# Routing lists written group by group, and the first expert's weight splits placed behind the routing

## The chip, the cores and the metric

The kernel runs on one core of one Trainium2 chip. The metric is the device time of one execution in microseconds (us). The engines are named as in the profile: PE multiplies matrices, DVE (vector), ACT (scalar) and POOL work on tiles in SBUF, and SP only issues DMAs. POOL issues the indirect DMAs (gathers and scatters by an index), which the profile lists as its instructions.

## The reference, cut to what matters

One block of a network on 2048 tokens of width 1024, all in float32: two mixers, then a mixture of experts. Only the part from the second norm on matters here.

```python
x = x + gt1 * (mixed @ w_out[l])
h2 = rmsnorm(x, norm2_g[l]) * (1.0 + sc2) + sh2
x = x + gt2 * hier_moe(h2, ...)          # and a last rmsnorm

# hier_moe: 4 groups of 8 experts, two experts for each token
lg = (xf @ wg_r) + bg_r                  # 4 group logits
grp_idx = top_k(lg, 1)
le = ((xf @ we_r) + be_r)                # 32 expert logits
pe = softmax(le of the chosen group)
top_p, top_i = lax.top_k(pe, TOP_K)
wts = p_grp * top_p / sum(top_p)
...
hid = silu(xblk @ w_gate[e]) * (xblk @ w_up[e])
yb = hid @ w_down[e]                     # for each expert and its tokens
out = out.at[buf_tok].add(yb * buf_w)
```

## The kernel before, in words

The program has three parts one after the other: the mixers, a middle part (class `Mid`), and the experts (class `Moe`). The change lies at the border of the last two.

**The middle part** goes over 16 tiles of 128 tokens. `Mid.tile(i)` multiplies a tile with `w_out` on PE (48 products of 128x512, because each float32 operand is split into a high and a low part and three of the four products are kept), scales the result on DVE (line 934, tile `wot`) and adds it to `x` (line 935, on POOL, for the last tile on DVE). `Mid.after(j)` stores `x`, transposes it on PE, copies the transposes on ACT (line 948), takes the sum of squares on ACT (line 951), the reciprocal root on DVE and POOL (`rsqrt_small`, lines 86 and 87, tile `xrs`), forms the 36 logits `lg` (line 956 on PE, line 957 on DVE) and the normed row `h` (lines 958 and 959 on DVE), which is stored to `H2`.

**The routing** (`route`) takes a group of tiles, `GROUPS = [(0, 4), (4, 4), (8, 4), (12, 2), (14, 1), (15, 1)]` as (first tile, count). It is a chain of some fifty short DVE instructions from `lg` to the two one-hot choices `E` and their sum `M` (line 1057), two small products on PE (lines 1062 and 1063) that count how many tokens went to each expert before, and then the destination index `di` (line 1073) for each of the two choices. For each tile of the group and each choice it writes 128 rows of 16 bytes into the DRAM tensor `LIST` with one indirect DMA from POOL (line 1081): 32 such writes in all.

**The weights.** An expert has 12 pieces of 128x1024 float32 (4 of gate, 4 of up, 4 of down), 512 KB each. `Moe.load_next` issues the load of the next piece into a `raw` buffer. `Moe.pump(n)` splits the next n pieces into high and low parts (`halves`, line 1239 on ACT into `whi`, line 1240 on DVE into `wlo`), and each split issues the next load. There are 7 `raw` buffers, 12 pairs of `whi` and `wlo`, and 8 more raw buffers (`raw2`) once the memory of the middle part is free. `Moe.first`, called behind `tile(15)`, issues 7 loads and splits all 12 pieces of expert 0, with 12 more loads.

**The order.** Up to the end of `Mid.run` a planner orders the instructions of each engine, by the place in the program and by its own estimate of times. From `Moe.run` on each engine goes in the order of the program. `Moe.run` reads the lists of experts 0 to 2 on SP (line 1371, which waits for all writes of `LIST`), clears three buffers `gx` (line 1376, which also waits for those writes, since the buffers lie in memory that the routing used), takes the counts, gathers the rows of expert 0, 1 and a second block of expert 0 (line 1244), transposes and splits them (lines 1255, 1260, 1261), issues 8 loads on ACT's DMA queue, and starts the loop over the experts. In expert 0's `block` the first two pieces are used, then the hook `mid` runs an extra block for expert 0's tokens past 128 (tiles `ih`, `il`), which uses all 12 pieces, and then its own block goes on.

Of the kernel before, what the change touches and what calls it, by code (L numbers as in the profile page):

```python
# [864 lines left out]
class Mid:  # L865
# [103 lines left out]
    def run(s, ctx):  # L969
        s.moe.lasting()  # L970
        s.k.md = s.t = ctx.enter_context(s.k.tc.tile_pool(name="md", bufs=1, side="right"))
        s.rows()
        s.consts()
        xs, n, due = s.xs, len(s.xs), []
        for i in range(n, 17):
            if i < 15:
                s.tokens(i + 1)
            if i < 16:
                xs[i] = s.tile(i)
            if i == 15:  # L980
                s.moe.first()
            for j in [j for j in sorted(xs) if j < i]:
                i0, c = [(i0, c) for i0, c in GROUPS if i0 <= j < i0 + c][0]
                if j == i0:
                    lg = s.t.tile([128, 4, 36], FP, name="lg", bufs=4)
                s.after(j, xs.pop(j), lg[:, j - i0])
                if j == i0 + c - 1:
                    due.append((i0, c, lg))
                if due and (j >= sum(due[0][:2]) - 1 + (0 if due[0][0] > 8 else 3)):
                    route(s.k, *due.pop(0), s.moe.ps)  # L990
        for d in due:
            route(s.k, *d, s.moe.ps)


def first_of_max(k, v, mx, n, name):
# [12 lines left out]

def route(k, i0, c, lg, ps):

    nc, md = k.nc, k.md
    T = lambda n, *sh: md.tile([128, 4, *sh], FP, name=n, bufs=4)[:, :c]
    gl, el = lg[:, :c, 0:4], lg[:, :c, 4:36]
    gm = T("gm"); nc.vector.tensor_reduce(gm, gl, AX.X, OP.max)
# [52 lines left out]
    for j, e in enumerate(E):  # L1067
        t = T("pt" + str(j), 32); nc.vector.tensor_tensor(t, pos, e, OP.mult)
        d = T("d" + str(j)); nc.vector.tensor_reduce(d, t, AX.X, OP.add)
        if j == 1:  # L1070
            nc.vector.tensor_tensor(d, d, aside, OP.add)
        di = md.tile([128, 4], I32, name="di" + str(j), bufs=4)[:, :c]
        nc.vector.tensor_copy(di, d)
        row = md.tile([128, 4, 4], FP, name="lrow" + str(j), bufs=4)[:, :c]
        rowi = row.bitcast(I32)
        nc.gpsimd.iota(rowi[:, :, 0], pattern=[[128, c]], base=i0 * 128, channel_multiplier=1)
        nc.gpsimd.iota(rowi[:, :, 1], pattern=[[128, c]], base=i0 * 128, channel_multiplier=1)
        nc.gpsimd.memset(row[:, :, 3], 0.0)
        nc.gpsimd.tensor_scalar(row[:, :, 2], W[j], 1.0, 0.0, op0=OP.mult, op1=OP.add)
        for i in range(c):  # L1080
            one = nc.gpsimd.indirect_dma_start(
                out=k.LIST, out_offset=bass.IndirectOffsetOnAxis(ap=di[:, i:i + 1], axis=0),
                in_=row[:, i], in_offset=None)

            for other in k.scat:
                k.tc.declare_no_dep(one.ins, other.ins, reason="other rows")
            k.scat.append(one)


class Moe:  # L1090
# [31 lines left out]
    def first(s):  # L1122

        for _ in range(min(s.RAW, len(s.todo))):
            s.load_next()
        s.pump(s.RING)

    def load_next(s, queue=None):
        if s.loaded < len(s.todo) and (s.summed or s.loaded < s.k.NE * 12):
# [231 lines left out]
    def run(s, O):  # L1361
        k, nc, tc = s.k, s.nc, s.tc
# [6 lines left out]
        rows = k.LIST[0:65536, :].rearrange("(e a p) c -> p e a c", e=32, p=128)  # L1369
        for e in range(min(NE, 3)):  # L1370
            nc.sync.dma_start(lists[:, e], rows[:, e, 0:4])
        more = {}

        s.gx = [s.t.tile([128, 1024], FP, name=f"gx{j}") for j in range(3)]
# [3 lines left out]
        def second(e):  # L1378

            more[e] = x = s.gx[2]  # L1380
            n = nc.values_load(s.cnt[0:1, e:e + 1], engines=[mybir.EngineType.Pool], min_val=0, max_val=2048)
            with tc.If(n > 128):
                s.gather(lists[:, e, 1], x)

        def first(e):
            x = s.gx[e % 2]
            s.gather(lists[:, e, 0], x)
            return x
        s.counts()
        xs = [first(0)]  # L1390
        if NE > 1:
            xs.append(first(1))
        hl = s.x_tiles()
        for q in range(2):
            s.x_split(s.x_turn(xs[0], q), *hl, q)
        for _ in range(s.LATE):
            s.load_next(nc.scalar)
        second(0)
        for e in range(NE):
            n = nc.values_load(s.cnt[0:1, e:e + 1], min_val=0, max_val=2048)  # L1400
# [49 lines left out]
        with tc.If(most > 128):  # L1450
            for e in (NE - 2, NE - 1):
                n = nc.values_load(s.cnt[0:1, e:e + 1], min_val=0, max_val=2048)
# [118 lines left out]
```

## Time and profile before

| what | us |
|---|---|
| median of 3 runs | 2954.5 |
| lowest and highest of the runs | 2951.3 and 2956.52 |
| the profiled execution | 2948.01 |
| its span from first to last instruction | 2946.2 |

The profiled execution has 1.8 us around its span. Its rows are in a section of their own below; times in them are counted from the start of the span. PE is the busiest engine (2724.7 us, 92% of the span), DVE follows with 2013.0 us (68%), and the DMA engines are busy nearly all of the time while the experts run.

### The profile page before, as it was taken

What the parts mean: (1) busy time and instruction counts of PE and PEld (TensorE: products, weight loads), DVE (VectorE), ACT (ScalarE), POOL (GpSimd) and SP (SyncE); (2) the same over time, 40 slices, a digit from 0 to 9 for tenths busy, and PEclk for the clock granted to TensorE, in tenths of its full rate; (3) what the DMA queues carried; (4) which work ended last, traced back from release to release, by engine and by line L of the source; (5) the groups of instructions that cost most, each with busy time, mean ns of one, the idle gap of its engine ahead of it and who ended that gap; (6) DMA issues with size and microseconds to landing.
All of it is one profiled execution on the core that took longest, in us unless ns stands there. A gap on an engine that the chain in (4) does not pass through costs nothing. (4 is left out here: it accounts for less than half of the span.)

```text
span 2946.2 us, 45527 instructions
## 1 busy us (share of the span) xinstructions
PE 2724.7 (92%) x15434; PEld 2245.7 (76%) x15434; DVE 2013.0 (68%) x4136; ACT 1274.6 (43%) x2183; POOL 798.2 (27%) x983
## 2 busy tenths in 40 slices
PE   6989999999999999999999999899958999999993
PEld 5767787878888888888888878688857777777772
DVE  6374775683676656587647886436565699988984
ACT  4333443342333523333333544322225577767763
POOL 2011322322332312342233343322341112111111
PEclk9989999999999999999999989999979999999996
DMA  8999775577565776566665767976448799999996
GB/s 268 305 335 286 236 236 166 181 240 230 158 209 183 235 240 206 179 219 206 203 198 172 233 207 255 345 271 216 144 151 257 272 364 367 362 331 370 366 320 249
DMA packets 460586, 734.25 MB, mean 249 GB/s; under 512 B 115553, under 2 KB 277345, under 8 KB 460242
## 3 DMA queue, kind: packets, MB, share of 16 engines
q1 hardware_dynamic: 448114, 696.68, 70.7%
q0 software_dynamic: 10976, 29.21, 4.3%
q10 hardware_dynamic: 1152, 4.19, 0.4%
q8 instruction: 164, 2.69, 0.4%
q14 instruction: 180, 1.47, 0.2%
HBM read 561.81 MB, written 175.00 MB: 250 GB/s over the span
## 5 line engine op out<-in xcount | busy, mean ns | idle before, releaser
L778 PE MATMUL mm<-hThi,w 128*128 128x512 f32 x1472 | 592.8, 403 | 16.0 <-ACT hThi L667 10.0
L780 PE MATMUL mm<-hThi,w 128*128 128x512 f32 x1472 | 589.5, 401 | 0.2 <-DVE w L761 0.2
L779 PE MATMUL mm<-hTlo,w 128*128 128x512 f32 x1472 | 588.2, 400 | 0.0
L1240 DVE TENSOR_TENSOR wlo<-raw,whi 128x1024 fp32r<-128x1024 f32 x404 | 483.0, 1252 | 45.3 <-ACT whi L1239 29.2
L1239 ACT CAST whi<-raw 128x1024 fp32r<-128x1024 f32 x408 | 405.6, 1057 | 204.0 <-PE U L931 47.9
L778 PEld LDWEIGHTS mm<-hThi,w 128*128 128x128 f32 x1472 | 280.4, 190 | 85.2 <-ACT hThi L667 10.1
L780 PEld LDWEIGHTS mm<-hThi,w 128*128 128x128 f32 x1472 | 280.4, 191 | 65.2 <-DVE w L761 6.6
L779 PEld LDWEIGHTS mm<-hTlo,w 128*128 128x128 f32 x1472 | 280.2, 190 | 57.4 <-DVE hTlo L668 0.7
L1340 POOL DMA_INDIRECT X<-y,lists x32 | 70.8, 2213 | 484.7 <-DVE y L1332 447.5
L243 DVE TENSOR_TENSOR pr<-Pl,Nl 128x2 f32<-128x2 f32 (+30 forms) x496 | 184.9, 373 | 11.7
L451 POOL TENSOR_TENSOR Xq<-h,kf 128x256 f32<-128x256 f32 x96 | 80.1, 834 | 379.7 <-ACT h L448 128.8
L761 DVE TENSOR_TENSOR w<-wraw,w 128x512 fp32r<-128x512 f32 x108 | 80.5, 746 | 106.6 <-ACT w L760 106.6
L760 ACT CAST w<-wraw 128x512 fp32r<-128x512 f32 x108 | 66.6, 619 | 163.4 <-DMA wraw<-in_w_in_dram 103.7
L244 DVE TENSOR_REDUCE Pl<-pr 128x1 f32<-128x2 f32 (+30 forms) x496 | 124.3, 251 | 12.6
L296 PE MATMUL xy<-UV,Gc 128*64 128x64 f32 (+1 forms) x1536 | 115.3, 225 | 3.0 <-ACT UV L305 3.0
L1270 PE MATMUL G<-whi,xh 128*128 128x512 f32 x256 | 104.1, 407 | 11.3 <-PEq L1413 8.6
L296 PEld LDWEIGHTS xy<-UV,Gc 128*64 128x64 f32 (+1 forms) x1536 | 97.2, 128 | 20.2 <-issue 5.9
L856 PE MATMUL mm<-hThi,w 128*128 128x512 f32 x256 | 104.1, 410 | 7.6 <-DMA w<-Ww_proj_b 2.6
L857 PE MATMUL mm<-hTlo,w 128*128 128x512 f32 x256 | 103.9, 406 | 2.6 <-DVE hTlo L668 2.6
L858 PE MATMUL mm<-hThi,w 128*128 128x512 f32 x256 | 102.3, 400 | 0.0
L1270 PE MATMUL G<-whi,xl 128*128 128x512 f32 x256 | 100.7, 393 | 0.0
L1270 PE MATMUL G<-wlo,xh 128*128 128x512 f32 x256 | 100.6, 393 | 0.0
(495 smaller groups left out, 5798.9 us busy)
## 6 DMA issues: line engine op xcount, KB each, us to landing
raw<-in_exp_w_gate_dram SPq DMA_DIRECT2D x126, 512.0 KB
raw<-in_exp_w_up_dram SPq DMA_DIRECT2D x126, 512.0 KB
raw<-in_exp_w_down_dram SPq DMA_DIRECT2D x124, 512.0 KB
w<-Whg SPq DMA_DIRECT2D x96, 512.0 KB
w<-Wgt SPq DMA_DIRECT2D x96, 512.0 KB
w<-Wrw SPq DMA_DIRECT2D x84, 512.0 KB
wraw<-in_w_in_dram SPq DMA_DIRECT2D x92, 256.0 KB
Whg<-w SPq DMA_DIRECT2D x32, 512.0 KB
```

The lines of the kernel that those rows point to most:

```text
L243: nc.vector.tensor_tensor(pv, Pl[:, :ni, :ns], Nl[:, :ns, t_][:, None, :].to_broadcast([128, ni, ns]), OP.mult)
L244: nc.vector.tensor_reduce(Pl[:, :ni, t_], pv, AX.X, OP.add)
L296: mm = lambda *a_, **kw: nc.tensor.matmul(*a_, skip_group_check=True, **kw)
L778: nc.tensor.matmul(pt, whi, hi[kk // 2][:, kk % 2], start=(kk == 0), stop=False)
L779: nc.tensor.matmul(pt, whi, lo[kk // 2][:, kk % 2], start=False, stop=False)
L780: nc.tensor.matmul(pt, wlo, hi[kk // 2][:, kk % 2], start=False, stop=(kk == 7))
L856: nc.tensor.matmul(pt, w[:, 0, kk], hi[o // 2][:, o % 2], start=(kk == 0), stop=False)
L857: nc.tensor.matmul(pt, w[:, 0, kk], lo[o // 2][:, o % 2], start=False, stop=False)
L858: nc.tensor.matmul(pt, w[:, 1, kk], hi[o // 2][:, o % 2], start=False, stop=(kk == 3))
L1239: s.nc.scalar.copy(hi, raw)
L1240: eng.tensor_tensor(lo, raw, hi.bitcast(FP), OP.subtract)
L1270: mm = lambda *a, **kw: nc.tensor.matmul(*a, skip_group_check=True, **kw)
```

## The change

It does four things. The routing of the groups of four tiles comes one tile behind the group's last tile instead of three, and with `while` instead of `if` several groups can be routed in one step. `route` no longer issues its writes of `LIST` itself but returns them; they are issued right behind the routing, except for tile 14, whose two writes come behind `after(15)`. `Moe.first` only issues its 7 loads; the 12 splits of expert 0 go into `Moe.run`, six ahead of the split of the gathered rows and six behind it. The 8 loads into `raw2` go from ACT's queue, behind the split of the gathered rows, to SP's, right behind the reads of the lists. With this, those 8 loads are pieces 7 to 11 of expert 0 and 0 to 2 of expert 1; before they were pieces 7 to 11 of expert 1 and 0 to 2 of expert 2.

```diff
--- before.py
+++ after.py
@@ -971,7 +971,7 @@
         s.k.md = s.t = ctx.enter_context(s.k.tc.tile_pool(name="md", bufs=1, side="right"))
         s.rows()
         s.consts()
-        xs, n, due = s.xs, len(s.xs), []
+        xs, n, due, rows = s.xs, len(s.xs), [], []
         for i in range(n, 17):
             if i < 15:
                 s.tokens(i + 1)
@@ -986,10 +986,13 @@
                 s.after(j, xs.pop(j), lg[:, j - i0])
                 if j == i0 + c - 1:
                     due.append((i0, c, lg))
-                if due and (j >= sum(due[0][:2]) - 1 + (0 if due[0][0] > 8 else 3)):
-                    route(s.k, *due.pop(0), s.moe.ps)
-        for d in due:
-            route(s.k, *d, s.moe.ps)
+
+                while due and (j >= sum(due[0][:2]) - 1 + (0 if due[0][0] > 8 else 1)):
+                    rows += route(s.k, *due.pop(0), s.moe.ps)
+                if j < 14 or j == 15:
+                    for r in rows:
+                        r()
+                    rows = []
 
 
 def first_of_max(k, v, mx, n, name):
@@ -1008,7 +1011,7 @@
 
 def route(k, i0, c, lg, ps):
 
-    nc, md = k.nc, k.md
+    nc, md, out = k.nc, k.md, []
     T = lambda n, *sh: md.tile([128, 4, *sh], FP, name=n, bufs=4)[:, :c]
     gl, el = lg[:, :c, 0:4], lg[:, :c, 4:36]
     gm = T("gm"); nc.vector.tensor_reduce(gm, gl, AX.X, OP.max)
@@ -1078,13 +1081,15 @@
         nc.gpsimd.memset(row[:, :, 3], 0.0)
         nc.gpsimd.tensor_scalar(row[:, :, 2], W[j], 1.0, 0.0, op0=OP.mult, op1=OP.add)
         for i in range(c):
-            one = nc.gpsimd.indirect_dma_start(
-                out=k.LIST, out_offset=bass.IndirectOffsetOnAxis(ap=di[:, i:i + 1], axis=0),
-                in_=row[:, i], in_offset=None)
-
-            for other in k.scat:
-                k.tc.declare_no_dep(one.ins, other.ins, reason="other rows")
-            k.scat.append(one)
+            def write(di=di[:, i:i + 1], row=row[:, i]):
+                one = nc.gpsimd.indirect_dma_start(
+                    out=k.LIST, out_offset=bass.IndirectOffsetOnAxis(ap=di, axis=0), in_=row, in_offset=None)
+
+                for other in k.scat:
+                    k.tc.declare_no_dep(one.ins, other.ins, reason="other rows")
+                k.scat.append(one)
+            out.append(write)
+    return out
 
 
 class Moe:
@@ -1123,7 +1128,6 @@
 
         for _ in range(min(s.RAW, len(s.todo))):
             s.load_next()
-        s.pump(s.RING)
 
     def load_next(s, queue=None):
         if s.loaded < len(s.todo) and (s.summed or s.loaded < s.k.NE * 12):
@@ -1369,6 +1373,8 @@
         rows = k.LIST[0:65536, :].rearrange("(e a p) c -> p e a c", e=32, p=128)
         for e in range(min(NE, 3)):
             nc.sync.dma_start(lists[:, e], rows[:, e, 0:4])
+        for _ in range(s.LATE):
+            s.load_next()
         more = {}
 
         s.gx = [s.t.tile([128, 1024], FP, name=f"gx{j}") for j in range(3)]
@@ -1391,10 +1397,11 @@
         if NE > 1:
             xs.append(first(1))
         hl = s.x_tiles()
+
+        s.pump(s.RING // 2)
         for q in range(2):
             s.x_split(s.x_turn(xs[0], q), *hl, q)
-        for _ in range(s.LATE):
-            s.load_next(nc.scalar)
+        s.pump(s.RING - s.RING // 2)
         second(0)
         for e in range(NE):
             n = nc.values_load(s.cnt[0:1, e:e + 1], min_val=0, max_val=2048)
```

## Rows read from the trace of the kernel before

**Rows 1.** The page's first line.

```profile
span 2946.2 us, 45527 instructions
```

**Rows 2.** Stages: window, length, busy PE, PEld, DVE, ACT, POOL, then clock, DMA share, GB/s.

```profile
2140.00:2165.20 25.20, 25.20 (x134) 21.45 (x133) 19.82 (x40) 9.64 (x14) 9.89 (x17) 1.00 0.55 182
2165.20:2182.50 17.30, 9.55 (x65) 8.82 (x63) 15.44 (x58) 7.90 (x14) 0.55 (x1) 0.69 0.97 352
2182.50:2205.40 22.90, 4.72 (x18) 4.21 (x18) 10.15 (x100) 0.42 (x2) 16.90 (x25) 0.50 0.06 18
2205.40:2214.50 9.10, 1.90 (x8) 1.58 (x9) 1.94 (x5) 0.58 (x1) 3.98 (x4) 0.50 0.42 103
```

**Rows 3.** Line 1081 on POOL by window: count, ns min/median/max, first and last start.

```profile
L1081 POOL DMA_INDIRECT LIST<-lrow,di x16: 954/958/1072, 2182.5 to 2202.9; - x16
...
L1081 POOL DMA_INDIRECT LIST<-lrow,di x8: 955/964/1070, 2132.3 to 2141.3; - x8
```

**Rows 4.** Timeline of POOL: start, length, engine, line, operation, [idle before, releaser].

```profile
2142.32 1.30 POOL L935 TENSOR_TENSOR raw<-raw,wot 128x512 f32<-128x512 f32 x1
...
2207.92 1.06 POOL L1244 DMA_INDIRECT gx<-H,lists  x1 [1.47 <-DMA lists<-LIST]
```

**Rows 5.** Timeline of SP: the reads of the lists.

```profile
2205.37 1.41 SPq L1371 DMA_DIRECT2D lists<-LIST  x3
```

**Rows 6.** Line 1240 on DVE, 2160 to 2176 us: the splits.

```profile
L1240 DVE TENSOR_TENSOR wlo<-raw,whi x9: 1205/1223/1225, 2161.6 to 2173.4; 128x1024 fp32r<-128x1024 f32 x9
```

**Rows 7.** Timeline of DVE from the last tile's add to its last index.

```profile
2169.56 0.69 DVE L935 TENSOR_TENSOR raw<-raw,wot 128x512 f32<-128x512 f32 x1
...
2176.94 0.25 DVE L957 SCALAR_TENSOR_TENSOR lg<-tr,xrs,rtb 128x36 f32<-128x36 f32 x1 [1.26 <-PE tr L956]
...
2178.68 1.22 DVE L959 TENSOR_TENSOR h<-h,B 128x1024 f32<-128x1024 f32 x1
...
2194.09 0.19 DVE L1057 TENSOR_TENSOR M<-E,E 128x32 f32<-128x32 f32 x1
...
2197.55 0.15 DVE L1073 CAST di<-d 128x1 int32<-128x1 f32 x1 [0.26 <-DVE d L1071]
```

**Rows 8.** Timeline of DVE: eleven routing steps of tiles 8 to 11, first and last.

```profile
2134.55 0.19 DVE L1026 TENSOR_REDUCE m<-le 128x4 f32<-128x32 f32 x1
...
2137.04 0.19 DVE L1034 SCALAR_TENSOR_TENSOR pq<-o1q,pe 128x32 f32<-128x32 f32 x1
```

**Rows 9.** Timeline of PE: the last product of stage one.

```profile
2164.82 0.40 PE L932 MATMUL Y<-whi,wlo 128*128 128x512 f32 x1
```

**Rows 10.** Timeline of PE: the start of the experts.

```profile
2212.61 1.95 PE L1255 MATMUL tr<-ident,gx 128*128 128x128 f32 x8 [16.28 <-DMA gx<-H,lists]
...
2220.55 0.50 PE L1270 MATMUL tr<-whi,il 128*128 128x512 f32 x1
```

**Rows 11.** Timeline of ACT and its DMA queue there.

```profile
2217.97 0.46 ACTq L1167 DMA_DIRECT2D raw<-in_exp_w_gate_dram  x1
2219.18 1.07 ACT L1260 CAST ih<-tr 128x512 fp32r<-128x512 f32 x2 [4.00 <-DMA raw<-in_exp_w_down_dram]
```

**Rows 12.** Timeline of DVE there, and five splits later.

```profile
2205.67 0.91 DVE L1376 MEMSET gx<- 128x1024 f32 x1 [7.97 <-DMA LIST<-lrow,di]
...
2214.48 1.42 DVE L1261 TENSOR_TENSOR xl<-tr,xh 128x512 fp32r<-128x512 f32 x2 [6.73 <-ACT xh L1260]
...
2219.80 1.29 DVE L1261 TENSOR_TENSOR il<-tr,ih 128x512 fp32r<-128x512 f32 x2 [3.90 <-ACT ih L1260]
...
2253.45 5.77 DVE L1240 TENSOR_TENSOR wlo<-raw,whi 128x1024 fp32r<-128x1024 f32 x5
```

**Rows 13.** Line 1244, the gathers of expert rows, over the whole span (columns as rows 3).

```profile
L1244 POOL DMA_INDIRECT gx<-H,lists x36: 985/1410/2057, 2207.9 to 2845.3; - x36
```

**Rows 14.** DMA queues, 2249 to 2250 us: packets, MB, share of 16 engines.

```profile
q0 software_dynamic: 51, 0.21, 53.3%
q1 hardware_dynamic: 47, 0.18, 47.3%
```

## The prediction

> **What bounds the kernel now.** The first view is the table of stages around the border between the middle part and the experts, since the change touches nothing else [rows 2]. To 2165.2 us PE is busy without a gap (25.20 of 25.20 us): it sets the pace, and DVE, POOL or DMA work saved there is worth nothing. Then PE has almost nothing to do for 49 us: 9.55, 4.72 and 1.90 us of work in stretches of 17.3, 22.9 and 9.1 us. So at this border a chain of waits sets the end, and what it gives up comes off the end, as long as the experts start with the same pieces loaded. The second view is the timeline of each engine through that gap, followed back from the first product of the experts:
> - PE waits for the gathered rows until 2212.61 [rows 10], POOL's gather (2207.92) for the lists [rows 4], SP's read of them (2205.37) for all writes of LIST [rows 5].
> - The writes are POOL's. Sixteen of the 32 stand in one train, first start 2182.5, last 2202.9, so 1.36 us apart and the last ending at 2203.9 [rows 3]. POOL is busy 16.90 of 22.9 us there [rows 2].
> - The train is late because tiles 8 to 15 all get their destinations on DVE in this gap, and DVE runs nine splits of 1.22 us in it first (2161.6 to 2173.4) [rows 6]. The last tile's add runs at 2169.56 though its product ended at 2165.22 [rows 9]; its logits come at 2176.94, its M at 2194.09, its last index ends at 2197.70 [rows 7].
>
> **The change part by part.** I follow tile 15 to the end of its writes, then expert 0's start.
>
> *Product to logits.* Without splits on DVE the scaling and the add follow the product at once: two of 0.69 us and a hop of 0.1, so x is whole at 2166.7 instead of 2170.25, 3.5 us sooner. From there to the logits took 6.7 us, with casts of the splits among ACT's work. The bounds of what that loses are 0 and 2.7 us; I take 2, because ACT still has the square and two copies to do. Logits at 2171.4, 5.5 sooner.
>
> *Logits to M.* It took 17.15 us, with the routing of three more groups and the normed row h on DVE in between. Undisturbed, eleven chained steps start within 2.49 us, one round trip to ACT included: 0.25 us each [rows 8]. I count 32 chained steps, 8.0 us, and add h, which the program has ahead of the routing, with two instructions of about 1.25 us [rows 7]: 10.5 us, so 6.6 us less. Bounds: 8.0 (h falls beside) to 15 (tile 14's routing and unexplained pauses of DVE stay).
>
> *M to the last index.* 3.6 us [rows 7], unchanged: two products, five short steps.
>
> *Last index to last write.* It took 6.2 us since five writes still stood in the train. With the twelve writes of tiles 8 to 13 gone earlier and tile 14's two done, tile 15's two remain, 1.27 each, the first from an index that is ready 0.5 us sooner: 1.9 us, so 4.3 less. If tile 14's stand right ahead it is 2.5 more.
>
> Sum so far: 5.5 + 6.6 + 4.3 = 16.4 us; the last write ends at 2187.5. Bounds: 7 (logits held, M at 15 us) and 20.
>
> *The writes that move.* Twelve writes of 1.27 us go into POOL's queue while PE runs tiles 14 and 15, ahead of adds and reciprocal roots there. The trace shows such a burst: eight writes, 2132.3 to 2142.3 [rows 3], held an add to 2142.32 [rows 4], and PE still had no gap [rows 2]. I cost them at nothing; the cover is that PE takes up the transposes only after the next tile's products, and if it were gone the price is up to the 10 us of a burst. The four writes of tiles 12 and 13 (5.1 us) can stand ahead of tile 15's reciprocal root; that is in the bound of 7.
>
> *Expert 0's start*, counted from SP's read of the lists (2205.37 before). Before: DVE's first clear at 0.3, the gather at 2.55, the rows on PE at 7.24, xl from 9.11 to 10.53, il at 14.43, the extra block's third product, which needs il, at 15.18 [rows 4, 5, 10, 12]. The first six splits now stand on DVE behind the clears, because these wait for the writes: two clears of 0.91 end at 2.3, and six splits at 5.77/5 = 1.15 us [rows 12] end at 9.2. ACT's casts run ahead of that. The rows come later by two things. POOL prepares the gather beside splits: gathers take from 0.985 to 2.057 us, median 1.410 [rows 13], and the one here, beside an idle DVE, took 1.06 [rows 4]; I add 0.4. And the 8 loads are issued by SP just ahead of the gather. Where both queues have work, they move 51 and 47 packets in a microsecond, 0.39 MB together [rows 14]. So the gather's 0.52 MB take 2.7 us instead of 1.35; part of that was latency before, and I add 0.7 (bounds 0 and 1.35). The rows arrive at 8.3, xl runs from 10.2 to 11.6, and the 9.2 above lies under it with 1 us to spare. Then six more splits, 6.9 us, stand ahead of il, which DVE starts at 18.5 instead of 14.43. PE waits for it: **4.1 us lost**. Bounds 2.5 (no delay of the rows) and 7 (late loads). Pieces 7 to 11 must land first: 2.6 MB plus three gathers of 0.52 at 0.39 MB/us from about 2.7 is 13.5, a microsecond to land, and the last split starts at 17.5: 3 us of cover.
>
> The Trainium skill speaks against splits beside the gather: "GPSIMD Engine Reference", section "1. Specifications", says that POOL's way into SBUF is shared with DVE and that DVE instructions with two SBUF inputs contend for it, as a split is. The spread of the gathers agrees [rows 13]. By the longest gather the sum would be 0.6 us worse than mine, without such contention 0.4 better.
>
> *The loads.* ACT's queue no longer issues eight loads (the last at 2217.97, ahead of ih at 2219.18 [rows 11]); ACT has six casts there instead, and DVE is later than either. Twelve loads fewer run before 2180; SP has nothing else to issue behind the lists. Both kernels have 27 pieces loaded when expert 0's own block starts to split expert 1: 20 loads of 0.52 MB and the gathers, 12 MB, are 31 us at 0.39, done at about 34; that block resumes at about 40. So the experts start with equal stock, and the shift reaches the end.
>
> Net: 16.4 - 4.1 = 12.3 us. The profiled execution took 2948.0 (span 2946.2 [rows 1] and 1.8 around it) and becomes 2935.7. The median of the runs shown is 6.5 higher, and I carry the difference over: 2954.5 - 12.3 = **2942.2**.
>
> **The rivals.**
> - *The planner leaves the destinations late.* PE's small products for tiles 8 to 13 stay behind tile 15's, because PE has no gap before. Then the train of 16 writes only begins when DVE, free of splits, gets to it: about 2171.5 instead of 2182.5, 11 us, and with 4.1 lost the gain is 7: 2947.5. For it: PE's full stage [rows 2]. Against it: the earlier place in the program, and eight writes that were issued in such a full stage [rows 3].
> - *The logits or M stay late* (writes of tiles 12 and 13 ahead of the root, or DVE's pauses): the bound of 7, less 4.1, a gain of 3: 2951.5.
> - *Slower: expert 0's rows queue behind its loads.* If the gather were served after all that SP has queued, it waits for 8 loads of 1.35 us, 10.8, and the loss becomes about 14, a gain of 2; if after the six that the first splits issue too, 18.9, the loss is 22 and the time 2960. It decides from a wait of about 13 us on. Against it: the even packets of the two queues [rows 14].
> - *The gap closes further* (h beside, no contention): 20 - 2.5 = 17.5: 2937.
>
> **How the numbers follow.** A measurement of this kernel can tell about 0.2%, 5.9 us. Chances: the forecast with its own range, 2938 to 2947, 0.60; late destinations 0.17; late logits 0.12; the slow one 0.06; the gap closes further 0.05. The range of 8 in 10 goes from 2937 to 2951. Faster by over 0.2% (under 2948.6) holds the forecast, the last case and most of the late destinations: 0.77. Slower (over 2960.4) is part of the slow case and of burst trouble: 0.05. Within: 0.18.
>
> **What would show it.** Right: four writes of line 1081 after 2175 and the rest before tile 15's logits; those at about 2171; SP's read at about 2189; a wait of PE of 4 us for il in the extra block, behind six splits. Wrong: PE gaps before 2165 behind POOL's adds; a train of 16 writes as before; the gathered rows more than 10 us behind the lists; a wait of ACT's casts for pieces 7 to 11; or the experts' stage longer than before, which would say that the stock was not equal.

## The result, and the profile after

The kernel changed takes **2969.7 us** (median of 5 runs, 2963.91 to 2972.29), the kernel before 2952.9 beside it (5 runs): a ratio of 1.0057 with a 95% interval of 1.0042 to 1.0072. It is slower by 16.8 us (12.4 to 21.3 by the interval) where 12.3 less were forecast. The profiled execution took 2972.29, with a span of 2970.5 us.

Upstream of the change this execution ran 5.1 us later than the one of before, with the same code (PE's first product with `w_out` at 1933.23 instead of 1928.10), so distances are compared, not times of day. Four marks carry the comparison: PE's last product of the middle part, SP's read of the lists, the first product with `il`, and the first add of an expert's result into X (POOL, line 1344, before 1340). Those adds on POOL, before and after:

```profile
2240.13 1.63 POOL L1340 DMA_INDIRECT X<-y,lists  x1 [19.63 <-POOLq L1415]
```

```profile
2260.03 1.63 POOL L1344 DMA_INDIRECT X<-y,lists  x1 [23.23 <-POOLq L1422]
```

| us between | before | after | forecast |
|---|---|---|---|
| last product and read of the lists | 40.55 [rows 5, 9] | 39.30 | 24 |
| read of the lists and first product with `il` | 15.18 [rows 5, 10] | 28.38 | 19.3 |
| read of the lists and first X add | 34.76 | 49.54 | 39 |

The border as a whole (last product to first X add) grew from 75.31 to 88.84 us, 13.5. PE's stage ahead of it, from the first product with `w_out` to the last, grew from 236.7 to 238.0, 1.2. Over kernels whose middle part is the same (changed, e4, e5, e6, e10) that stage takes 237.4 to 239.4 us, so the 1.2 isn't clear of noise. The rest of the 16.8, some 2 us, I can't place; the interval is wider than that.

The stages of the border, laid as in [rows 2] (window, length, busy PE, PEld, DVE, ACT, POOL, then clock, DMA share, GB/s):

```profile
2146.30:2171.50 25.20, 25.20 (x140) 21.60 (x138) 14.26 (x49) 5.59 (x9) 7.78 (x10) 1.00 0.28 105
2171.50:2188.80 17.30, 7.35 (x33) 6.76 (x32) 10.02 (x50) 3.68 (x7) 8.90 (x12) 0.58 0.27 92
2188.80:2210.50 21.70, 7.96 (x34) 7.33 (x34) 9.85 (x74) 1.58 (x4) 4.92 (x10) 0.50 0.08 25
2210.50:2240.00 29.50, 8.88 (x33) 6.93 (x34) 18.20 (x20) 9.10 (x11) 12.11 (x5) 0.62 0.94 352
```

PE is still without a gap in the 25.2 us ahead of the border, so the moved writes of LIST don't hold it there. In the two stages behind it PE does 15.3 us of work in 39 us, and in the third row no engine is busy for half of the time. The gap is as long as before, with less work of DVE, ACT and POOL in it: a chain of waits. The timeline of PE names it (start, length, engine, line, operation, then idle time before and its releaser):

```profile
2171.19 0.39 PE L932 MATMUL Y<-whi,wlo 128*128 128x512 f32 x1
...
2175.20 0.60 PE L1065 MATMUL tr<-M,before 128*128 128x32 f32 x2 [3.62 <-DVE M L1060]
...
2176.47 1.95 PE L947 MATMUL tr<-ident,raw 128*128 128x128 f32 x8
...
2179.38 3.61 PE L956 MATMUL tr<-rtw,h2T 128*128 128x36 f32 x16
...
2191.30 0.61 PE L1065 MATMUL tr<-M,before 128*128 128x32 f32 x2 [8.31 <-DVE M L1060]
...
2192.15 1.95 PE L947 MATMUL tr<-ident,raw 128*128 128x128 f32 x8
...
2193.97 3.63 PE L956 MATMUL tr<-rtw,h2T 128*128 128x36 f32 x16
...
2203.96 0.60 PE L1065 MATMUL tr<-M,before 128*128 128x32 f32 x2 [6.36 <-DVE M L1060]
...
2227.76 1.96 PE L1259 MATMUL tr<-ident,gx 128*128 128x128 f32 x8 [21.84 <-DMA gx<-H,lists]
...
2238.87 0.74 PE L1274 MATMUL tr<-whi,il 128*128 128x512 f32 x1 [1.59 <-DVE il L1265]
```

Read the lines 947 and 956: these are the transposes and logits of tile 14 (2176.47) and tile 15 (2192.15). Each stands behind a product of line 1065, which counts the tokens of the group routed before and waits for that group's M. Tile 15's `x` was whole at 2173.0, as the timeline of DVE shows, but it was transposed only at 2192.15, behind the M of tile 14 (2190.96):

```profile
2172.34 0.69 DVE L935 TENSOR_TENSOR raw<-raw,wot 128x512 f32<-128x512 f32 x1
...
2174.82 0.23 DVE L1060 TENSOR_TENSOR M<-E,E 128x64 f32<-128x64 f32 x1
...
2190.96 0.19 DVE L1060 TENSOR_TENSOR M<-E,E 128x32 f32<-128x32 f32 x1
...
2197.64 0.26 DVE L957 SCALAR_TENSOR_TENSOR lg<-tr,xrs,rtb 128x36 f32<-128x36 f32 x1 [3.91 <-PE tr L956]
...
2203.63 0.19 DVE L1060 TENSOR_TENSOR M<-E,E 128x32 f32<-128x32 f32 x1
...
2206.22 0.15 DVE L1076 CAST di<-d 128x1 int32<-128x1 f32 x1
...
2212.79 6.88 DVE L1244 TENSOR_TENSOR wlo<-raw,whi 128x1024 fp32r<-128x1024 f32 x6
...
2231.31 6.90 DVE L1244 TENSOR_TENSOR wlo<-raw,whi 128x1024 fp32r<-128x1024 f32 x6 [0.25 <-ACT whi L1243]
...
2238.13 1.28 DVE L1265 TENSOR_TENSOR il<-tr,ih 128x512 fp32r<-128x512 f32 x2
```

So three routing chains run in series: M of tiles 12 and 13 at 2174.82, of tile 14 at 2190.96, of tile 15 at 2203.63. POOL's timeline shows that the writes of LIST, no longer a train [rows 3], wait for them, and then the second loss, the first gather (the last two lines are a write and that gather):

```profile
2175.44 0.96 POOL L1085 DMA_INDIRECT LIST<-lrow,di  x1 [0.30 <-issue]
...
2181.78 1.06 POOL L1085 DMA_INDIRECT LIST<-lrow,di  x1 [4.32 <-issue]
...
2194.16 1.01 POOL L1085 DMA_INDIRECT LIST<-lrow,di  x1 [3.31 <-DVE di L1076]
...
2208.11 0.96 POOL L1085 DMA_INDIRECT LIST<-lrow,di  x1 [0.30 <-issue]
...
2213.17 7.43 POOL L1248 DMA_INDIRECT gx<-H,lists  x1 [1.43 <-DMA lists<-LIST]
```

Eight writes end at 2176.4, four begin at 2181.78, two at 2194.16, the last one ends at 2209.1, and SP reads the lists at 2210.49.

The gather that took 1.06 us [rows 4] took 7.43 here, and it ended 0.9 us behind the sixth of six back-to-back splits (2212.79, 6.88 us). Its rows then reached PE 7.2 us later (2220.60 to 2227.76) instead of 3.6. The DMA queues in three stretches of one microsecond, 1.0, 3.0 and 4.0 us behind its end (q0 is POOL's, q1 SP's; packets, MB, share):

```profile
q1 hardware_dynamic: 117, 0.43, 105.0%
...
q1 hardware_dynamic: 86, 0.29, 71.4%
...
q0 software_dynamic: 33, 0.14, 32.8%
...
q0 software_dynamic: 54, 0.22, 53.7%
...
q1 hardware_dynamic: 50, 0.20, 47.8%
```

For three microseconds nothing of the gather moves (the two stretches not shown have packets of q1 alone, too), in the fourth it has a third of the bytes, and in the fifth the two queues share evenly. Before, with no loads ahead, the gather's first packets came within 0.8 us of its end.

### The profile page after: what moved, and what is told of

Same layout as the page of the kernel before. It is cut to its first block, busy times and chain, and to the rows that moved or that the text cites. A ratio compares the mean times of both kernels' runs of the same rounds, so it can differ in the third digit from the quotient of the medians.

```text
span 2970.5 us, 45543 instructions
## 1 busy us (share of the span) xinstructions
PE 2729.7 (92%) x15434; PEld 2244.8 (76%) x15434; DVE 2018.6 (68%) x4136; ACT 1274.6 (43%) x2183; POOL 806.2 (27%) x983
## 5 line engine op out<-in xcount | busy, mean ns | idle before, releaser
L778 PE MATMUL mm<-hThi,w 128*128 128x512 f32 x1472 | 594.3, 404 | 15.1 <-ACT hThi L667 10.2
L778 PEld LDWEIGHTS mm<-hThi,w 128*128 128x128 f32 x1472 | 281.5, 191 | 84.8 <-ACT hThi L667 10.2
L244 DVE TENSOR_REDUCE Pl<-pr 128x1 f32<-128x2 f32 (+30 forms) x496 | 124.2, 250 | 12.6
```

Source lines behind the costliest of these rows:

```text
L244: nc.vector.tensor_reduce(Pl[:, :ni, t_], pv, AX.X, OP.add)
L778: nc.tensor.matmul(pt, whi, hi[kk // 2][:, kk % 2], start=(kk == 0), stop=False)
```

## The experiments

Times are medians beside the kernel before on the same chip, with the ratio and its 95% interval; the ratio isn't the quotient of the two medians and differs from it by up to 0.12%. "Tail" is last product to read of the lists, "start" is the read to `il`'s first product, "border" is last product to first X add.

| run | tail | gather | start | border | median us (before) | ratio |
|---|---|---|---|---|---|---|
| before | 40.55 | 1.06 | 15.18 | 75.3 | | |
| changed | 39.30 | 7.43 | 28.38 | 88.8 | 2969.7 (2952.9) | 1.0057 [1.0042, 1.0072] |
| e1_routing_only | 48.85 | 1.06 | 16.31 | 84.7 | 2961.9 (2953.5) | 1.0037 [1.0025, 1.0050] |
| e2_splits_only | 35.43 | 7.42 | 27.81 | 82.8 | 2959.0 (2953.5) | 1.0020 [1.0005, 1.0034] |
| e3_own_bank | 28.31 | 7.32 | 28.45 | 76.5 | 2953.9 (2953.5) | 1.0011 [0.9995, 1.0027] |
| e4_splits_behind_rows | 37.45 | 1.05 | 29.41 | 88.2 | 2969.3 (2953.5) | 1.0054 [1.0026, 1.0082] |
| e5_loads_on_act | 39.37 | 7.34 | 28.67 | 89.9 | one execution, 2971.2 | |
| e6_broken_train | 38.99 | 7.43 | 28.60 | 88.8 | one execution, 2967.2 | |
| e7_own_bank_splits_early | 35.65 | 1.06 | 16.09 | 71.3 | 2949.8 (2951.1) | 0.9999 [0.9981, 1.0016] |
| e8_own_bank_splits_last | 35.36 | 1.06 | 16.33 | 71.3 | 2951.3 (2951.1) | 0.9997 [0.9984, 1.0010] |
| e9_spread | 32.23 | 1.05 | 15.62 | 67.4 | 2946.9 (2953.0) | 0.9985 [0.9968, 1.0002] |
| e10_train_waits | 37.43 | 1.76 | 22.85 | 79.8 | one execution, 2958.2 | |
| e11_splits_beside_writes | 32.67 | 1.05 | 15.58 | 67.8 | 2951.8 (2951.6) | 0.9996 [0.9978, 1.0014] |
| e12_spread_waits | 30.95 | 1.06 | 16.69 | 68.8 | 2946.4 (2951.6) | 0.9971 [0.9958, 0.9985] |

Tail, gather, start and border are each from one profiled execution. The tail's code is the same in the kernel changed, e4, e5, e6 and e10, and their tails go from 37.43 to 39.37: two tails that differ by less than 2 us can't be told apart.

**The two halves apart.** e1 takes the routing of the change and leaves splits and loads as they were; e2 the reverse.

```diff
 # e1, against the kernel changed: Moe.first
             s.load_next()
+        s.pump(s.RING)
 # Moe.run: both pumps and SP's 8 loads out, the 8 loads on ACT's queue back in
```

> Only the routing and its list writes are as in the changed kernel; splits and loads are where they were before. Two distances are read: tail, from the last product with w_out to SP's read of the lists (40.6 us before, 39.3 changed), and start, from that read to the extra block's first product with il (15.2 before, 28.4 changed). Theory of the start (splits and loads behind the lists are what lengthened it): start is back at 15, so about 13 us better than the changed kernel and near the kernel before. Theory that the tail is a chain in series (on PE the transposes of a tile stand behind the count products of the group routed ahead of it): tail stays at 39 or grows by the splits' share, up to 45. Rival for the tail (DVE's splits were what held it): tail grows by well over 5, since the splits are back on DVE.

> Only the splits and the eight loads are moved; the routing and its writes are as before. Theory of the start: start is about 28 as in the changed kernel. The tail shows what DVE gains when the nine splits are gone, with the 16 writes still in one train: if the tail was set by DVE, it is 30 (11 us shorter, the train begins at once); if by something in series, 36 to 40.

Each half alone is slower than before, by 0.37% and 0.20%; neither covers for the other. e1's tail of 48.85 lies beyond the 45 of the chain theory, where its rival had it, and e2's 35.43 lies between its two cases: DVE's splits and the routing's new order both have a share in the tail, and these two runs alone don't divide it. The routing lengthens the tail by 8.3 us, although it starts the writes earlier: with the splits back on DVE the M of tiles 12 and 13 is there at 2182.45, tile 14's at 2195.75, tile 15's at 2208.42, so what delays the first chain delays all three. The splits shorten the tail by 5.1 when they leave, and lengthen the start by 12.6.

**The shared banks.** The tiles `tr` of the transposes, the logits and the counts share four PSUM buffers. e3 gives the counts of the last three groups a bank of their own.

```diff
-    pt = ps.tile([128, 512], FP, name="tr", bufs=4)
+    pt = (k.pg.tile([128, 512], FP, name="G", bufs=1) if i0 >= 12 else
+          ps.tile([128, 512], FP, name="tr", bufs=4))
```

> The changed kernel, with the count products of the last three groups in a bank of their own (G) instead of one of the four that the transposes and logits take in turn. Serial theory (the turn of the shared banks puts tile 14's and 15's transposes behind the counts of the groups before them): the transposes now come right behind the last product, tile 15's logits 5 to 8 us behind it instead of 26, and the tail falls from 39 to about 23 to 27; start unchanged at 28; the whole 12 to 16 us better than the changed kernel. Rival (the chain of routing and the writes set the tail whatever the order on PE): tail stays near 39.

The tail falls from 39.30 to 28.31 us, a little above the 23 to 27 expected, and the time from 0.57% over before to 0.11% (14 us by the ratios, 16 by the medians). PE's timeline in e3, and tile 15's logits on DVE there:

```profile
2170.42 0.64 PE L948 MATMUL tr<-ident,raw 128*128 128x128 f32 x4
...
2174.00 1.92 PE L957 MATMUL tr<-rtw,h2T 128*128 128x36 f32 x8 [2.95 <-ACT h2T L949]
...
2177.01 1.90 PE L957 MATMUL tr<-rtw,h2T 128*128 128x36 f32 x8
...
2185.90 0.60 PE L1067 MATMUL G<-M,before 128*128 128x32 f32 x2 [6.57 <-DVE wt L1047]
```

```profile
2178.95 0.26 DVE L958 SCALAR_TENSOR_TENSOR lg<-tr,xrs,rtb 128x36 f32<-128x36 f32 x1 [0.61 <-PE tr L957]
```

Tile 15's transposes (2170.42) and logits (2177.01) now stand ahead of the counts of tile 14 (2185.90) and tile 15 (2187.41); M of 14 and 15 come 1.1 us apart (2185.52 and 2186.64) instead of 12.7. That shows the cause of 11 us of the tail: the order on PE, behind the shared buffers, put the chains in series. It isn't all: tile 15's logits come 12.30 us behind the last product (2166.65) here, where 5 to 8 were expected, and the kernel before had 12.1. ACT begins to copy tile 15's transposes at 2173.36, 2.3 us behind the last of them; on POOL its reciprocal root stands behind a train of eight writes of LIST and starts at 2172.34, 2.4 us after its input; and the counts of tiles 12 and 13 stand between the two halves of its logits on PE. Which of these sets the 12.30 no run separates.

**The first gather.** In the changed kernel two things are new beside it: six splits on DVE and a burst of loads on SP. e4 puts all twelve splits behind the rows; e5 puts the eight loads back on ACT's queue behind the rows.

```diff
 # e4
-        s.pump(s.RING // 2)
         for q in range(2):
             s.x_split(s.x_turn(xs[0], q), *hl, q)
-        s.pump(s.RING - s.RING // 2)
+        s.pump(s.RING)
 # e5
-        for _ in range(s.LATE):          # SP, behind the lists
-            s.load_next()
+        for _ in range(s.LATE):          # behind x_split
+            s.load_next(nc.scalar)
```

> The changed kernel, with all twelve splits behind the split of the gathered rows, so that DVE runs none while POOL prepares the gathers; SP's burst of eight loads stays where it is. In the changed kernel the first gather takes 7.43 us on POOL, against 1.06 before. If the splits on DVE hold it: 1.0 to 1.1 here. If SP's burst of loads holds it: about 7 again. Rows on PE at about 8 to 11 us behind the lists' read in the first case (17.3 in the changed kernel); then il comes behind twelve splits of 1.15, at about 24 to 27, so the start is 25 to 28 and the whole 0 to 3 us better than the changed kernel.

> The changed kernel, with the eight loads on ACT's queue behind the split of the gathered rows, as they stood before the change; the six splits still stand ahead of those rows. If the splits alone hold POOL's first gather, it takes 7.3 to 7.5 us again; if it takes both the splits and SP's burst, about 1 to 2. The time from the end of that gather on POOL to the rows on PE was 3.6 us before, 7.2 changed and 7.8 with the splits behind: if the loads ahead of the gather in the queues cause that, it is 3.6 to 5 here (the six loads that the splits issue remain).

The two causes come apart. POOL's line in e4 and then in e5:

```profile
2206.20 1.05 POOL L1248 DMA_INDIRECT gx<-H,lists  x1 [1.43 <-DMA lists<-LIST]
```

```profile
2213.97 7.34 POOL L1248 DMA_INDIRECT gx<-H,lists  x1 [1.52 <-DMA lists<-LIST]
```

Without splits beside it the gather takes 1.05 us, with SP's burst still there; without the burst it takes 7.34, with the splits still there. So the splits hold POOL's preparation. From the end of the gather to PE it is 7.75 us in e4 and 3.76 in e5 (7.2 in the kernel changed, 3.6 before): the loads ahead in the DMA queues cost 3.4 to 4.1. In e4 as in the kernel changed 1.2 to 1.3 MB of loads move between the end of the gather and its first packets (some 3.4 and 3.2 us behind it), although in e4 only 1.5 MB of the eight loads' 4.2 have moved by then: the gather waits for a part of what is queued ahead, not for all of it. What sets that part no run shows. Neither run helps the time: in e4 `il` stands behind 12 splits (13.7 us), and the start is 29.41, over the 25 to 28 expected; in e5 eight load issues and six casts stand ahead of the cast to `ih` on ACT (2236.91).

**Why this gather and not the others.** Among the experts gathers take 1.0 to 2.1 us [rows 13], also beside equally dense splits. There a semaphore instruction, a wait for another engine, stands ahead of each split on DVE; in the train at the start none does. e6 puts a one-column clear between the splits, e10 a one-column add whose operands come from PE and ACT.

```diff
 # e6
+            s.pump(1)
+            nc.vector.memset(gap, 0.0)
 # e10
+            nc.tensor.matmul(pq[:, 32 * i:32 * i + 32], k.ones, k.Msum, start=True, stop=True)
+            nc.scalar.copy(ga[:, i:i + 1], k.Msum[:, 0:1])
+            nc.vector.tensor_tensor(gb[:, i:i + 1], pq[:, 32 * i:32 * i + 1], ga[:, i:i + 1], OP.add)
+            s.pump(1)
```

> The changed kernel with a clear of one column on DVE behind each of the first six splits, some 0.1 us each. Among the experts gathers of 1.0 to 2.1 us run beside trains of splits, and there a semaphore instruction stands ahead of each split; at the start six splits run with none between them. If POOL gets its turn wherever another instruction stands between two splits, the first gather takes 1 to 3 us and the rows come 4 to 6 us sooner than in the changed kernel. If any row of splits holds it, it takes 7.5 to 8 again.

> The kernel changed, with a small add of two columns ahead of each of the first six splits, whose operands come from PE and from ACT, so that DVE has an instruction that waits for two engines between two splits, as it has among the experts, where gathers beside six dense splits took 1.0 to 2.1 us. Theory: POOL's preparation of a gather is let in at such a wait of DVE: the first gather takes 1 to 3 us, although the splits stay as dense. Rival: the dense splits hold it whatever stands between them: 7.4 to 8.5 us, as with a one-column clear between them (7.43); then what sets the experts' gathers apart is something else, and stays open.

DVE in e6, then POOL there:

```profile
2207.46 0.06 DVE L1404 MEMSET gap<- 128x1 f32 x1
...
2208.59 1.21 DVE L1244 TENSOR_TENSOR wlo<-raw,whi 128x1024 fp32r<-128x1024 f32 x1
...
2209.74 1.21 DVE L1244 TENSOR_TENSOR wlo<-raw,whi 128x1024 fp32r<-128x1024 f32 x1
```

```profile
2206.74 7.43 POOL L1248 DMA_INDIRECT gx<-H,lists  x1 [1.49 <-DMA lists<-LIST]
```

DVE in e10, then POOL there:

```profile
2209.21 1.20 DVE L1244 TENSOR_TENSOR wlo<-raw,whi 128x1024 fp32r<-128x1024 f32 x1
...
2210.34 0.14 DVE L1407 TENSOR_TENSOR gb<-tr,ga 128x1 f32<-128x1 f32 x1
...
2210.41 1.20 DVE L1244 TENSOR_TENSOR wlo<-raw,whi 128x1024 fp32r<-128x1024 f32 x1
```

```profile
2209.59 1.76 POOL L1248 DMA_INDIRECT gx<-H,lists  x1 [1.50 <-DMA lists<-LIST]
```

In both the splits start 1.14 to 1.20 us apart. A clear that needs nobody changes nothing (7.43 us); with the add the gather is through in 1.76, and the start is 22.85 instead of 28.38. The add doesn't hold DVE up: its operands were ready, and DVE has no idle time before it. It brings two things, a semaphore instruction on DVE and a read of PSUM, and the two runs don't tell these apart. The kernel changed does. Behind the rows it runs six more splits, as dense as the first six (6.90 us from 2231.31 on) and with both inputs in SBUF, but with a semaphore instruction ahead of each. Line 1244 on DVE from 2229 to 2240 (count, ns min/median/max, first and last start; DVEq is DVE's queue), then POOL there:

```profile
L1244 DVEq EVENT_SEMAPHORE  x6: 21/21/21, 2230.4 to 2235.1; - x6
```

```profile
2235.05 1.75 POOL L1248 DMA_INDIRECT gx<-H,lists  x1 [11.86 <-DVE wlo L1244]
```

The gather beside this train took 1.75 us, and those beside the second trains of e2, e3, e5 and e6, built the same way, took 1.07 to 2.06. For the first six splits the same view lists no semaphore instruction. So the wait alone is enough, without PSUM; why POOL gets in at it no run shows.

**Putting the parts together.** e7 and e8 keep e3's bank, with the loads as before and the splits early (as before) or last in the middle part.

> The routing of the changed kernel with the counts of the last three groups in a bank of their own, and splits and loads where they were before the change. Start as before, 15 to 16 us. Tail: 28 with the splits gone from DVE; with nine splits (11 us) back on DVE in it 31 to 37, if they are partly under waits for PE. Whole: 3 to 9 us better than the kernel before. If the tail is 40 or more, the splits take their whole time.

> As the one before, but the twelve splits stand behind the whole routing in the middle part, so that the planner gives them the lowest rank there. Tail 29 to 34, start 15 to 16, whole 6 to 11 us better than the kernel before, if rank keeps them off the routing's chain; the same as the one before, if the planner fills DVE's waits with them all the same.

The start is back (16.1 and 16.3), but the tail is 35.4 to 35.7, not 28.3: with nine splits cut into it, DVE's chain is 7 us longer, and the time is that of before. In e8 the planner moved the splits forward into the chain, so the two kernels are nearly one; of the 3 to 11 us expected of them nothing came. e9, e11 and e12 divide the twelve splits.

```diff
 # e9, against e7 (loads left out): Moe.first, Moe.run ahead of the lists, behind x_split
-        s.pump(s.RING)
+        s.pump(5)
+        s.splits(6)            # splits without their loads
+        s.splits(1)
 # e11: 5, 5 and 2; each of the middle five behind a one-column copy of the last index
+            eng.tensor_copy(lo[:, 0:1], s.k.last)
 # e12: 6; behind the first gather 4, each behind an add as in e10; 2
+        nc.gpsimd.memset(gp, 0.0)      # behind the first gather; the adds write gp, too
```

> The counts of the last groups in a bank of their own, as before this run; the twelve splits of expert 0 divided by where DVE has nothing else to do: five are offered early (they run between two tiles, before 2158), six stand ahead of the two clears, where DVE idled 5.4 us waiting for the writes, and one stands behind the rows. Their loads go out behind them: four on SP ahead of the lists, eight on ACT's queue behind the rows, three on SP within the first expert. Theory: the two losses are separate, the tail's is PE's order behind the shared banks plus splits that cut into DVE's chain, the start's is splits beside the gather and loads ahead of it. Then the tail is 28.3 to 30 us (28.31 with its own bank and no splits in it, 40.55 before), the first gather 1.1 to 1.5 us, the rows on PE 7.3 to 8.5 us behind the lists and il's first product 15 to 17 behind, and the time is some 10 us under before, 2940 to 2944. Rival: what the splits cost, they cost anywhere in this gap: tail 35 us as with all splits early, or the start over 20, and a time within 0.2% of before.

e9's splits did not stay where I had put them: the planner had eight of the eleven start between 2163.75 and 2174.39, so the tail is 32.23, 3.9 above that without splits. The start is as good as before, and the time, 0.15% under before, has an interval that still holds 1.

> As e9_spread, but now five splits are tied to the last index (a one-column copy of it ahead of each) and so stand exactly where DVE waits for the last list writes; five are offered early, two stand behind the rows. They lie beside POOL's last writes of LIST, which POOL prepares as it does a gather. Theory (dense splits with no wait for another engine between them hold POOL's preparation until they end): the writes that are left when the last index is there, two to four of 1.27 us, are held to the end of the splits, about 6 us, and the lists are read 33 to 35 us behind the last product, no better than 32.23 with splits early, although the last index comes sooner, 23 us behind the last product (26.2 there). Rival (only gathers are held, a write of 16 bytes a row is not): the lists are read 28 to 29.5 us behind the last product, and the time is 3 us under e9_spread's.

The tail is 32.67, near what the theory had, but not for its reason. POOL's last writes and SP's read of the lists:

```profile
2196.52 2.00 POOL L1089 DMA_INDIRECT LIST<-lrow,di  x1 [0.31 <-DVE wlo L1257]
...
2200.14 1.02 POOL L1089 DMA_INDIRECT LIST<-lrow,di  x1 [0.30 <-issue]
```

```profile
2206.03 0.93 SPq L1392 DMA_DIRECT2D lists<-LIST  x2
```

One write took 2.00 us, the others 1.0: the splits hardly held them. The last index came 22.7 us behind the last product, the last write ended at 2201.2, and only then something is late: the read stands 4.9 us behind it, against 1.4 in the kernel changed (2209.1 to 2210.49). SP had issued four loads from 2197.71 on, and the writes' bytes had to get through the DMA queues beside them. By my estimate, without these 3.5 us, the tail would be 29.2, where the rival had put it. But the run doesn't decide between the two: the copy put a semaphore instruction ahead of each of the five splits, so the theory's condition, splits with no wait between them, wasn't met. That POOL was let in fits e10; whether the writes are held less than gathers was not tried apart.

> Own bank for the last counts; six splits offered early, four behind the first gather (they wait for POOL to be past it), each behind a small add that waits for PE and ACT, and two behind the rows; loads behind them. This takes each place where splits were seen to cost least. Theory: the first gather takes 1.0 to 1.3 us, the next two 1.8 to 2.2; the four splits end about 9.5 us behind the lists, the rows' xl starts at 9.4 to 10.5, il's first product comes 15.5 to 17 behind the lists; the lists are read 29 to 31 us behind the last product, since one or two splits less cut into DVE's chain than in e9_spread (32.23). Time 2942 to 2946, 0.25 to 0.4% under before. Rival: four splits behind the gather hold the two others and the rows of the extra block come late, il 18 or more behind the lists: no better than e9_spread.

POOL and DVE in e12:

```profile
2200.04 1.06 POOL L1256 DMA_INDIRECT gx<-H,lists  x1 [1.72 <-DMA lists<-LIST]
...
2201.40 2.03 POOL L1256 DMA_INDIRECT gx<-H,lists  x1 [0.18 <-issue]
```

```profile
2201.26 0.16 DVE L1414 TENSOR_TENSOR gp<-tr,ga 128x1 f32<-128x1 f32 x1 [1.65 <-POOL gp L1405]
...
2204.99 1.21 DVE L1252 TENSOR_TENSOR wlo<-raw,whi 128x1024 fp32r<-128x1024 f32 x1
```

The splits lie between the first gather and the rows, where DVE has nothing else; the second gather takes 2.03 us and nobody waits for it. The tail came 1.3 us under e9's, which is within the spread of one code. The time is 0.29% under before by the ratio (2946.4 against 2951.6 us by the medians, 0.18%), the only one of the six versions with the bank whose interval lies on the fast side. It beats the kernel changed clearly and the one before by little.

Where this gain comes from isn't shown. e11's border is 1 us shorter than e12's, and its time is that of before; e7 and e8 take 4 us off the border and nothing clear off the time. Gains of 4 to 8 us at the border are hardly larger than the intervals here (4 to 5 us to either side), so taken together these runs don't show that they reach the end in full, as the prediction took for granted.

## Why the prediction was wrong, point by point

- **Product to logits** (forecast 5.5 us sooner): the step that failed. `x` was whole 1.8 us behind the last product, as forecast (1.9), but the logits came 26.45 us behind it instead of 6.6 (12.1 before). I freed tile 15 of DVE's splits and did not ask what stands ahead of its transposes on PE: the counts of tiles 12 to 14, whose place in the program the change had moved forward, and which share four buffers with them. Of the 20 us by which the logits missed, that is 14: with the counts in a bank of their own they came 12.30 us behind the product (e3). The other 6 were too hopeful in any case, and their cause stays open; e3 has the same splits gone from DVE and is no sooner than before. The rival of late logits named the right place, but from other causes, POOL's writes and DVE's pauses, and its gain of 7 in the tail was still too high.
- **Logits to M** (10.5): 5.99 us. The steps cost 0.20 us each, below the 0.25 taken [rows 8], and `h` fell beside. Right in kind and long in size; but three such chains run one behind the other.
- **M to the last index, and to the last write**: 2.7 us (3.6 forecast), then 4.1 from the index to SP's read (3.4 forecast, 1.9 and 1.5 until the read). Right.
- The tail in sum: 1.25 us gained instead of 16.4, less than the spread of one code and so nothing to speak of, which makes some 15 of the error of 29. The rival of late destinations expected the train of writes to stay; the train went, and the time with it into waits for M.
- **The writes that move** cost PE nothing, but this is in part luck: eight of the twelve started only at 2166.38, 4.8 us ahead of the last product, and the other four behind it (2181.78), so they hardly met the stage that they were to stand in. The eight stood ahead of tile 15's reciprocal root, which I had feared of the other four.
- **Expert 0's start** (4.1 lost): 13.2 lost, two terms mis-sized. The gather beside the splits was put at 0.4 us and cost 6.4. I took the spread of the experts' gathers for a bound [rows 13], and there a wait for another engine stands ahead of each split. The loads ahead were put at 0.7 with a bound of 1.35 and cost 3.5: the sharing of the two queues [rows 14] begins only three microseconds behind the gather's end. The third term held: from the rows on PE to `il` it took 10.4 us, 10.2 were forecast.
- The rival on the slow side (rows behind loads, 22 us lost, 2960) had the right place and the wrong price: the gather waited for 1.3 MB of the loads and not for all of them, the DMA queues gave 3.5 us of the loss, and the larger part was POOL's preparation, which no rival named.
- **The loads and the stock**: from the first X add to the last it is 672.5 us after and 668.3 before, and 665.8 to 677.2 over all the runs, so nothing can be said of the stock from it.

The Trainium skill was right in the place where I gave it least weight: "GPSIMD Engine Reference", section "1. Specifications", has POOL's interfaces shared with DVE instructions of two SBUF inputs; the gather's 7.43 us beside the splits and 1.05 without them agree. The Trainium skill's "SBUF — State Buffer", section "SBUF: two separate sides", calls the shared pair an exclusive lock that is held for the whole instruction, by whichever engine starts first (for a DVE instruction with two SBUF inputs, only against a POOL instruction that reads SBUF). By that alone a gather would wait for one split at a time; here it waited for the whole train of six (7.43 us), and for about one where a semaphore instruction stood between the splits (1.75 and 1.76). The measurement decides.

The Trainium skill's "DMA: Bandwidth & Descriptors", section "Queues, rings and completion order", says that a DMA engine goes round its queues packet by packet. The even shares of the fifth microsecond (54 and 50 packets) agree. By that alone the gather would have had its share from its first packet on; for three microseconds it had none, and the measurement decides.

## What to carry to other kernels

Before a producer is moved forward, follow its consumers' queue on every engine and the buffers they share: an early small product that waits can stand ahead of a late one that is on the path, and three short chains in series cost more than one long train (4 us of tail without splits on DVE, 8 with them). A stretch where DVE idles isn't free if POOL prepares an indirect DMA in it; put splits such as these behind the gather, or see that a wait for another engine stands between them. Take the price of an operation from rows in which its neighbours also wait as they will, not from rows that only look as dense.

## What was not expected of the hardware

- Six DVE subtractions of 128x1024 without a wait between them held the preparation of a gather from 1.06 to 7.43 us (7.32 to 7.43 in five kernels). A clear of one column between them left it at 7.43; an add with operands from PE and ACT made it 1.76, and beside six equally dense splits with a semaphore instruction ahead of each it took 1.07 to 2.06, also in five kernels.
- A gather of 0.52 MB behind queued loads of 512 KB sent no packet for three microseconds, while 1.3 MB of the loads moved, and then shared: its rows came 7.2 us behind its end, against 3.6 with empty queues and 3.76 with the loads issued later.
- Behind a stage with PE busy without a gap at a granted clock of 1.00, the clock was 0.58 and then 0.50, the lower level of 1.2 GHz, in the gap (0.69 and 0.50 before [rows 2]). The logits of tile 15, sixteen products, took 3.63 us there, in the series; sixteen such products took 1.87 ahead of the gap in before's trace. So PE's waits here also doubled the time of the few products between them. The sixteen in before:

```profile
2157.32 1.87 PE L956 MATMUL tr<-rtw,h2T 128*128 128x36 f32 x16
```
